# Second parts of weights by a ScalarE negation and an accumulating DMA in place of a subtraction, between the two layers of a decoder trunk

## The chip, the core and the metric

The program runs on one core of a Trainium2 chip. The metric is the device time of one execution in microseconds (us), lower is better. The engines are TensorE (PE in the rows, PEld for its weight loads), VectorE (DVE), ScalarE (ACT), GpSimd (POOL) and SyncE (SP, which only issues DMAs here). Each engine takes its instructions in the order in which they stand in its queue and waits at each for the semaphores that the instruction needs.

## What is computed

A trunk of two layers over 1024 tokens of 1024 channels, float32. Each layer is a token mixer and a squared-ReLU MLP with a hidden width of 4096, both behind an RMSNorm whose scale, shift and gate come from a conditioning vector. Layer 0 mixes with a recurrent block, layer 1 with a causal pooling mixer.

```
for i in (0, 1):
    h = rms_norm(x, g_mix[i]) * (1 + scale_m) + shift_m
    y = recurrent_mixer(h) if i == 0 else pool_mixer(h)
    x = x + gate_m * y
    h = rms_norm(x, g_ffn[i]) * (1 + scale_f) + shift_f
    u = relu(h @ w1[i])
    x = x + gate_f * ((u * u) @ w2[i])
return rms_norm(x, g_final)

# pool_mixer: four groups of 256 channels, windows of 2, 4, 8, 16 tokens
pooled = trailing_mean(h, window) - h
mixed = pooled @ w_pool[group]            # 256 x 256 each, times pool_scale
```

## The kernel before

The tokens are cut into two halves of 512 and the channels into blocks of 128, so that every tile is 128 partitions by 512 tokens. All weights and activations that TensorE takes are in two float32r parts that add up to the float32 value: a high part (the value cast to float32r) and a low part (the value less its high part). A product of one weight block with one activation block is three matmuls, all in `mm3`: high by high (L178), high by low (L179), low by high (L180).

A weight tile `w_...` of the pool `wpool` (eight buffers) holds both parts of 128x512 weights. A unit of 128x1024 weights is loaded by one DMA of SP into a `raw_...` tile (`load`, L99, three buffers) and made into two such tiles by `split_part`: ScalarE casts (L170), and GpSimd or VectorE, by the argument `eng`, subtracts (L171). A cast can run as soon as the last matmul that reads the buffer's former weights is through.

```
def split_part(raw, name, eng=None):
    w, n = split_tile(name), raw.shape[-1]
    S.copy(w[:, 0, 0:n], raw)                                                   # L170
    (eng or V).tensor_sub(w[:, 1, 0:n], raw, w[:, 0, 0:n].bitcast(F32))         # L171
    return w
```

Between the layers the halves of the tokens are run one behind the other, so that TensorE has the MLP of one half to do during the norm and the windows of the other. The order in which the program is written there is: `f2_fast(0, 6)` in two parts (`f2_weights_one`, then `f2_weights_two`), `f1` and `f2` of chunk 7 for the first half, `pool_windows(0)` spread as side work over the next products, `f1(0, 7, (1,))`, `pool_mix(0)`, `f2(0, 7, (1,))` with `ffn_norm(1, 0)` as side work, `pool_windows(1)` over `f1(1, 0, (0,))` and `f2(1, 0, (0,))`, `pool_mix(1)`, `f1(1, 1, (0,))` with `ffn_norm(1, 1)`, `f1(1, 0, (1,))`, `f2(1, 0, (1,))`. `f1` and `f2` are the first and second product of the MLP, with `f1_block` making the two parts of the squared hidden channels (`relu` L620, `usq` L625, `u` L609 and L610).

From that the framework's scheduler makes one fixed order for each engine and sets the semaphores; the order within a queue is not changed while the program runs. It puts casts far ahead of their use, as far as the eight buffers allow.

Names that the prediction uses: `pool_windows` makes the trailing sums `pw` (L900; windows of 16 on GpSimd, the others on VectorE), `pooled` (L907, L909, L910, L939), and the parts `ph` (ScalarE, L914) and `pl` (VectorE, L915). `SumSq.add` squares a block on ScalarE (L252) and adds it to a running sum on VectorE (L253: `ssqf1a`, `ssqn0b`, `ssqf1b`), which TensorE adds up over the partitions (L262). `norm_split` makes `hh` and `hl` (L284 to L291, three of eight `hl` on GpSimd at L288). `add_scaled` of `f2_fast` adds on GpSimd (L779).

Of the kernel before, what the change touches and what calls it, by code (L numbers as in the profile page):

```python
# [10 lines left out]
F32 = mybir.dt.float32  # L11
F32R = mybir.dt.float32r
AF = mybir.ActivationFunctionType
ALU = mybir.AluOpType
# [14 lines left out]
# Columns of the packed per-channel vectors, eight columns (one per block of channels) each.  # L29
# [13 lines left out]
def trunk_kernel(ctx, tc, xT, vecs, wmod, w_k, w_in, w_y, w_g, w_out, w_p, w1, w2, outT):  # L43
# [16 lines left out]
    class Blocks:  # L60
        """Eight blocks of channels of one half of the tokens, in two slots"""
# [41 lines left out]
    # The weights of the first products, in the order in which they are used: two blocks of rows  # L103
    # of six blocks of the input projection, and the conditioning's blocks of columns.
    mod_raw, k_raw = {}, []

    def piece(r, q, part):
        """Columns of a part of r, which is halved for the first two blocks of rows."""
        n = r.shape[-1] // (2 if q == 0 else 1)
        return part * n, part * n + n  # L110
# [29 lines left out]
    # silu(c) as a row on every partition  # L140
    cs = const.tile([P, NB], F32, name="cs")
    with tc.issue_after(S.activation(cs, vcol("c"), AF.Sigmoid).ins):
        # has the table of the first norm's square root loaded ahead of it
        S.activation(const.tile([P, 1], F32, name="early"), eps, AF.Sqrt)
# [3 lines left out]
    for n in range(2):  # L148
        ps = small_ps()
        # the columns of cs on diagonals, whose sums over the partitions are on every partition  # L150
        dg = tmp("dg").rearrange("p (q i) -> p q i", i=P)
        V.tensor_mul(dg, ident[:, None, :].to_broadcast([P, 4, P]),
                     cs[:, 4 * n:4 * n + 4, None].to_broadcast([P, 4, P]))
        PE.matmul(out=ps, lhsT=ones, rhs=dg, start=True, stop=True)
        cond_copy.append(S.copy(cond[:, n * H:(n + 1) * H], ps))
# [4 lines left out]
    def split_unit(src, name, eng=None, drips=None):  # L160
        raw = load(src, name)
        drip(rate[0] if drips is None else drips)
        return [split_part(raw[:, c:c + H], f"{name}_{c}", eng) for c in (0, H)]
# [10 lines left out]
    def mm3(ps, unit, col, rh, rl, first, last):  # L174
        """ps += unit[:, col:col+128].T @ (rh + rl)"""
        w, c = unit[col // H], col % H
        wh = w[:, 0, c:c + P]
        PE.matmul(out=ps, lhsT=wh, rhs=rh, start=first, stop=False)  # L178
        PE.matmul(out=ps, lhsT=wh, rhs=rl, start=False, stop=False)  # L179
        PE.matmul(out=ps, lhsT=w[:, 1, c:c + P], rhs=rh, start=False, stop=last)  # L180

    def proj(unit, hh, hl):
        """One 128-row block of W.T @ h for one token half, K = 1024."""
        ps = acc_mm()
        for k in range(NB):
            mm3(ps, unit, k * P, hh[:, k, :], hl[:, k, :], k == 0, k == NB - 1)
        return ps

# [6 lines left out]
    def mod_column(m, e, raw):  # L195
        """m[:, e] = raw @ cond"""
        V.scalar_tensor_tensor(raw, raw, 1.0, cond, op0=ALU.mult, op1=ALU.mult, accum_out=m[:, e:e + 1])  # L197
# [8 lines left out]
    def mod_steps():  # L206
        """The rest of the conditioning in small steps, taken between those of the other work."""
# [19 lines left out]
    def norm_scale(g, m, name):  # L227
        """g * (1 + scale)"""
# [5 lines left out]
    class SumSq:  # L234
        """Sums of squares of n tokens: up to three partial sums, added up by the tensor engine."""
# [19 lines left out]
    def rstd_bcast(ss, trace=None):  # L255
        """PSUM tile [P, n] with 1/sqrt(mean + eps) of every token on every partition."""
# [10 lines left out]
        # in two float32r parts on diagonals, whose sums over the partitions are on every partition  # L267
# [38 lines left out]
    # Six blocks of the input projection take the channels of the first half of the tokens  # L306
    # as the conditioning of each 128 of them is ready.
# [8 lines left out]
    def after(f, *args, **kw):  # L316
        """Issues behind what the last call on the same engine issued."""
# [7 lines left out]
    def column(dst, j, k, scale, first):  # L325
        """dst[:, k] = first + scale * (conditioning of channel block k)"""
# [16 lines left out]
    def prepare(q, part=0):  # L343
        """The float32r parts of the weights of two blocks of rows, or of one if q is 0"""
# [126 lines left out]
    # coefficient of the gate in log a: 8 * log_sigmoid(lambda)  # L471
# [17 lines left out]
    # log1p(z) = 2 s (1 + po)  # L489
# [11 lines left out]
    def gates(hd, unit, h):  # L501
        """RG-LRU of one head; its states take the place of its input."""
# [16 lines left out]
        for mi in range(2):  # L519
            b = 2 * hd + mi  # L520
            # a = exp(log a);  1 - a^2 = (1 + a^2) * tanh(-log a)
# [77 lines left out]
    # U[c]: the hidden channels of chunk c, in slots of two blocks each: (first or last two blocks,  # L599
    # half of the tokens), and the sums of them that the second product of the MLP takes  # L600
# [3 lines left out]
    def f1_block(unit, j, h, u, fast):  # L604
# [7 lines left out]
        def minus(a, n):  # L612
            """a less a block that is there in its two parts"""
# [15 lines left out]
        # for f2_fast the halves of the tokens change places  # L629
# [33 lines left out]
    class Ahead:  # L663
        """Units of weights, which are prepared one ahead of those in use"""
# [11 lines left out]
    # pieces of the conditioning by unit of a chunk of the MLP  # L676
# [8 lines left out]
    def f1(i, c, halves, by_half=False, eng=None, side=iter(()), fast=False, ahead=None):  # L685
        """`side` is other work, a step of which is traced after each unit.

        `fast` is set where f2_fast takes the result: "in turn" if one half of the tokens is done before the other.
        """
# [22 lines left out]
    def f2_weights(i, c, r, eng=None):  # L712
        """The parts of blocks of rows r and r + 4 of W2.T for f2_fast, by the product that takes them"""
# [18 lines left out]
    def f2_weights_one(i, c, r, eng):  # L732
        """Those of f2_weights for the products that the first half of the tokens takes"""
# [12 lines left out]
    def f2_weights_two(i, c, r, eng):  # L746
        """The others"""
        raw = rawp.tile([P, D + 256], F32, tag="raw", name=f"raw_w2_{i}_{c}_{r}")[:, 0:H]
        nc.sync.dma_start(raw, w2[i, c, r, :, 256:768])
        w = split_part(raw, "a12_a22", eng)  # L750
        return {2: (w, 0, (1, 0)), 4: (w, 256, "t4")}

    def f2_fast(i, c, ahead, products=(1, 5, 6, 3, 7, 2, 4), side=iter(())):
        """The second product of the MLP by Winograd's form of Strassen's seven products.

        W2.T is cut into two blocks of rows r, r + 4 by the first and last two hidden blocks, and the
        hidden channels into the latter by the halves of the tokens.
        """
# [52 lines left out]
        for r in range(4):  # L811
            # the last block of hidden channels is of use to the last two only
# [4 lines left out]
    # blocks of columns of a unit of w2, by block of rows of the product  # L817
# [22 lines left out]
    def once(fn):  # L840
        """Work of a single step"""
        fn()
        yield
# [3 lines left out]
    def jobs(i, first, last):  # L847
        """The units of chunks that run one after the other"""
# [14 lines left out]
    # 1 / min(t + 1, window) for the first 16 tokens  # L863
# [9 lines left out]
    def pool_windows(h, ss):  # L873
# [3 lines left out]
        def normed(k, hx, scale=1.0):  # L877
            """scale * (normalized and modulated x), after the last 15 tokens of the half before"""
# [46 lines left out]
        def ahead(k):  # L925
            if k < 6:
                hxs[k] = tmp("hx", W)
                # windows of two need only half the difference of neighbours, none for the first token
# [22 lines left out]
    def pool_mix(h, parts, out_ss):  # L951
        ph, pl = parts
        up = [split_unit(w_p[q], f"p{q}", G) for q in range(2)]
# [11 lines left out]
    # The first half of the tokens runs ahead of the second through the pooling mixer,  # L965
    # so that the tensor engine has one half's MLP to do during the other's norms and windows.
# [10 lines left out]
    f1(0, 7, (0,))  # L977
    f2(0, 7, (0,), sa)
    side = pool_windows(0, sa)
    f2_fast(0, 6, Ahead([partial(f2_weights_two, 0, 6, r, G) for r in range(4)]), (2, 4), side)  # L980
    f1(0, 7, (1,), eng=G, side=side)
# [3 lines left out]
    f2(0, 7, (1,), sb, eng=G, side=once(lambda: ffn_norm(1, 0, qa)))  # L985
    side = pool_windows(1, sb)
    f1(1, 0, (0,), eng=G, side=side)
    f2(1, 0, (0,), eng=G, side=side)
# [3 lines left out]
    f1(1, 1, (0,), eng=G, side=once(lambda: ffn_norm(1, 1, qb)), fast="in turn")  # L992
    f1(1, 0, (1,), eng=G)
    f2(1, 0, (1,))
# [28 lines left out]
    def mid_norm():  # L1023
        """The middle piece's final norm on GpSimd, which leaves VectorE to the last piece."""
# [19 lines left out]
def _layout(inputs):  # L1044
    """The arrays of the launch: the inputs, cut into the tiles that the kernel loads."""
# [28 lines left out]
    # two blocks of rows each: of the first 512 columns, then of the next 256  # L1074
# [3 lines left out]
    # two blocks of rows of the product each, r and r + 4  # L1078
# [34 lines left out]
```

## Time and profile before

| what | value |
|---|---|
| median of 3 runs | 1798.73 us (1798.16 to 1800.46) |
| span of the profiled execution | 1797.3 us |
| TensorE busy | 1718.5 us, 96% |
| VectorE busy | 1419.8 us, 79% |
| ScalarE busy | 913.7 us, 51% |
| GpSimd busy | 585.9 us, 33% |
| bytes moved by DMA | 158.76 MB, 88 GB/s over the span |

The profiled execution has no time beside its span; the median of the runs is 1.4 us longer than that span. Shares over the whole span say little here: between 360 and 990 us and from 1170 us on TensorE is nearly never idle, and what other engines save there is worth nothing. What counts is the stage between the layers, from about 990 to 1170 us, which is read by windows, waits and single instructions. A window's row gives its length, then for TensorE, its weight loads, VectorE, ScalarE and GpSimd the busy time and, in brackets, how many instructions ran; then the granted TensorE clock as a share of its upper level (1.00 is 2.4 GHz, 0.50 is 1.2 GHz), the busy share of the 16 DMA engines and GB/s.

### The profile page before, as it was taken

The page shows a single profiled execution, that of the slowest core. Times are in us where ns is not written, and L with a number is a line of the kernel's source. Part 1 is how long each engine was busy: PE and PEld are TensorE (multiplying, and loading weights), DVE is VectorE, ACT ScalarE, POOL GpSimd, SP SyncE. Part 2 cuts the span into 40 slices and gives each one's busy share as a digit, 9 for nine tenths or more (in the row PEclk, how much of TensorE's full clock was granted, in tenths as well). Part 3 has the DMA queues.
Part 4 walks back from the last instruction along what each step waited for, and adds up shares of the span by engine and source line. Part 5 has one row for each costly group of instructions (what it writes and reads, how often), then busy time and mean ns, then how long its engine had stood idle before and what let it go on. Part 6 is the DMA issues. An engine that isn't in the chain of part 4 may idle for free.

```text
span 1797.3 us, 20872 instructions
## 1 busy us (share of the span) xinstructions
PE 1718.5 (96%) x7510; PEld 1405.2 (78%) x7510; DVE 1419.8 (79%) x2124; ACT 913.7 (51%) x1558; POOL 585.9 (33%) x434
## 2 busy tenths in 40 slices
PE   6899989989999999999999988999999999999997
PEld 4687768778788888888888766788887787878787
DVE  8997866678888889898876897958787878686836
ACT  4588884255454444545454464445444444545422
POOL 5323341242322414151324655511322324041403
PEclk8999989989999999999999988999999999999999
DMA  9223314521424233242213221231202111121202
GB/s 363 73 84 109 136 47 142 162 83 59 136 70 134 73 115 106 94 126 73 83 58 106 81 72 59 83 105 51 70 33 71 36 59 52 42 61 46 71 13 94
DMA packets 47479, 158.76 MB, mean 88 GB/s; under 512 B 5008, under 2 KB 7440, under 8 KB 47376
## 3 DMA queue, kind: packets, MB, share of 16 engines
q1 hardware_dynamic: 47376, 157.43, 26.9%
q8 instruction: 59, 0.97, 0.2%
q14 instruction: 44, 0.36, 0.1%
HBM read 153.21 MB, written 4.19 MB: 88 GB/s over the span
## 4 chain that ended last, share of the span: by engine, by line
PE 62%; DVE 22%; ACT 5%; issue 5%; DMA 4%; POOL 2%; DVEq 0%; SPq 0%; ACTq 0%; POOLq 0%
PE mm L178 20%; PE mm L179 20%; PE mm L180 20%; DMA mb<-in_wmod 3%; DVE mb L197 2%; DVE xa L770 1%; DVE mw L323 1%; POOL xa L779 1%; DVE pw L900 1%; DVE xb L770 1%; DVE xca L439 1%; PE sm L262 1%; DVE hl L291 1%; DVE w_a_s L171 1%; DVE xcb L439 1%
## 5 line engine op out<-in xcount | busy, mean ns | idle before, releaser
L178 PE MATMUL mm<-hh,w_w 128*128 128x512 f32 x1024 | 401.4, 392 | 0.9 <-DVE xa L770 0.9
L180 PE MATMUL mm<-hh,w_w 128*128 128x512 f32 x1024 | 400.9, 392 | 0.0
L179 PE MATMUL mm<-hl,w_w 128*128 128x512 f32 x1024 | 400.6, 391 | 0.0
L779 POOL TENSOR_TENSOR xb<-xb,c 128x512 f32<-128x512 f32 x104 | 150.4, 1446 | 632.1 <-ACT c L774 564.4
L178 PEld LDWEIGHTS mm<-hh,w_w 128*128 128x128 f32 x1024 | 193.5, 189 | 42.8 <-DVE xa L770 2.7
L180 PEld LDWEIGHTS mm<-hh,w_w 128*128 128x128 f32 x1024 | 193.6, 189 | 40.3
L179 PEld LDWEIGHTS mm<-hl,w_w 128*128 128x128 f32 x1024 | 193.5, 189 | 40.0
L779 POOL TENSOR_TENSOR xa<-xa,c 128x512 f32<-128x512 f32 x104 | 160.3, 1542 | 145.1 <-ACT c L774 145.1
L774 ACT ACTIVATE c<-c,mod 128x512 f32<-128x512 f32 x104 | 75.3, 724 | 209.7 <-DVE c L800 119.8
L197 DVE SCALAR_TENSOR_TENSOR mb<-mb,cond 128x1024 f32<-128x1024 f32 x80 | 113.8, 1423 | 55.2 <-DMA mb<-in_wmod 54.6
L620 ACT ACTIVATE relu<-mm 128x512 f32<-128x512 f32 x128 | 76.2, 595 | 152.4 <-PE mm L180 143.6
L170 ACT CAST w_w<-raw_w 128x512 fp32r<-128x512 f32 x192 | 113.5, 614 | 63.2 <-PE mm L180 50.6
L171 DVE TENSOR_TENSOR w_w<-raw_w,w_w 128x512 fp32r<-128x512 f32 x136 | 130.5, 967 | 16.8 <-ACT w_w L170 16.7
L770 DVE SCALAR_TENSOR_TENSOR xa<-mm,mod,xa 128x512 f32<-128x512 f32 x156 | 112.9, 741 | 16.6 <-POOL xa L779 16.6
L171 POOL TENSOR_TENSOR w_w<-raw_w,w_w 128x512 fp32r<-128x512 f32 x56 | 83.5, 1498 | 71.6 <-ACT w_w L170 62.6
L179 PE MATMUL mm<-u,w_w 128*128 128x512 f32 (+1 forms) x224 | 81.4, 363 | 1.7 <-DVE u L610 1.7
L178 PE MATMUL mm<-u,w_w 128*128 128x512 f32 (+1 forms) x224 | 80.8, 364 | 1.7 <-ACT u L609 1.7
L180 PE MATMUL mm<-u,w_w 128*128 128x512 f32 (+1 forms) x224 | 81.0, 362 | 0.0
L178 PE MATMUL mm<-u,w_a_a 128*128 128x512 f32 x200 | 79.1, 396 | 1.9 <-DVE xa L770 1.0
L610 DVE TENSOR_TENSOR u<-usq,u 128x512 fp32r<-128x512 f32 x102 | 72.9, 715 | 8.5 <-ACT u L609 7.5
L770 DVE SCALAR_TENSOR_TENSOR xb<-mm,mod,xb 128x512 f32<-128x512 f32 x104 | 77.0, 741 | 2.6 <-PE mm L180 2.2
L179 PE MATMUL mm<-u,w_a_a 128*128 128x512 f32 x200 | 78.0, 390 | 0.0
(332 smaller groups left out, 4078.3 us busy)
## 6 DMA issues: line engine op xcount, KB each, us to landing
raw_w<-in_w SPq DMA_DIRECT2D x148, 512.0 KB, 3.6
mb<-in_wmod SPq DMA_DIRECT2D x80, 512.0 KB, 3.6
mw<-in_wmod SPq DMA_DIRECT2D x16, 512.0 KB, 9.6
raw_in<-in_w_in SPq DMA_DIRECT2D x8, 512.0 KB, 3.7
raw_y<-in_w_y SPq DMA_DIRECT2D x8, 512.0 KB, 3.6
raw_o<-in_w_out SPq DMA_DIRECT2D x8, 512.0 KB, 3.7
outT<-o SPq DMA_DIRECT2D x12, 256.0 KB, 2.4
xa<-in_xT SPq DMA_DIRECT2D x4, 512.0 KB, 5.4
```

The lines of the kernel that those rows point to most:

```text
L170: S.copy(w[:, 0, 0:n], raw)
L171: (eng or V).tensor_sub(w[:, 1, 0:n], raw, w[:, 0, 0:n].bitcast(F32))
L178: PE.matmul(out=ps, lhsT=wh, rhs=rh, start=first, stop=False)
L179: PE.matmul(out=ps, lhsT=wh, rhs=rl, start=False, stop=False)
L180: PE.matmul(out=ps, lhsT=w[:, 1, c:c + P], rhs=rh, start=False, stop=last)
L197: V.scalar_tensor_tensor(raw, raw, 1.0, cond, op0=ALU.mult, op1=ALU.mult, accum_out=m[:, e:e + 1])
L439: V.scalar_tensor_tensor(o, xr[:, k:k + H], vcol(f"cw{k}", m), o, op0=ALU.mult, op1=ALU.add)
L610: eng.tensor_sub(u[n][:, 1, jj, :], src, u[n][:, 0, jj, :].bitcast(F32))
L620: S.activation(r, ps, AF.Relu)
L770: V.scalar_tensor_tensor(xb, ps, g[:, r + 4 * row:r + 4 * row + 1], xb, op0=ALU.mult, op1=ALU.add)
L774: S.activation(t, src, AF.Identity, scale=g[:, r + 4 * row:r + 4 * row + 1])
L779: G.tensor_add(xb, xb, t)
```

## The change

For 84 of the weight tiles the low part is no longer a subtraction. ScalarE writes the high part as before, then writes its negative into the low part's place, and a DMA issued from GpSimd's queue reads the same weights from HBM a second time and adds them there: low = -high + value. The DMA is 256 KB, 128 rows of 2 KB. It waits for the negation, and the matmuls at L180 wait for its landing. Sixty of the 84 tiles had their subtraction on GpSimd, and 24 (chunk 7's `f1` and `f2` for the first half of the tokens, and `f2(1, 0, (1,))`) on VectorE. Beyond these tiles nothing changes its arithmetic. Comments and docstrings are taken out as well, and lines from `neg_part` on stand ten further down in the changed kernel.

```diff
+    def neg_part(raw, src, name):
+        w, n = split_tile(name), raw.shape[-1]
+        S.copy(w[:, 0, 0:n], raw)
+        S.activation(w[:, 1, 0:n], w[:, 0, 0:n].bitcast(F32), AF.Identity, scale=-1.0)
+        nc.gpsimd.dma_start(w[:, 1, 0:n], src, accum_op=ALU.add)
+        return w
     def split_unit(src, name, eng=None, drips=None):
         raw = load(src, name)
         drip(rate[0] if drips is None else drips)
+        if eng == "dma":
+            return [neg_part(raw[:, c:c + H], src[:, c:c + H], f"{name}_{c}") for c in (0, H)]
         return [split_part(raw[:, c:c + H], f"{name}_{c}", eng) for c in (0, H)]
...
-    def f2_weights_two(i, c, r, eng):
+    def f2_weights_two(i, c, r):
...
-        w = split_part(raw, "a12_a22", eng)
+        w = neg_part(raw, w2[i, c, r, :, 256:768], "a12_a22")
...
-        up = [split_unit(w_p[q], f"p{q}", G) for q in range(2)]
+        up = [split_unit(w_p[q], f"p{q}", "dma") for q in range(2)]
...
-    f1(0, 7, (0,))
-    f2(0, 7, (0,), sa)
+    f1(0, 7, (0,), eng="dma")
+    f2(0, 7, (0,), sa, eng="dma")
     side = pool_windows(0, sa)
-    f2_fast(0, 6, Ahead([partial(f2_weights_two, 0, 6, r, G) for r in range(4)]), (2, 4), side)
-    f1(0, 7, (1,), eng=G, side=side)
+    f2_fast(0, 6, Ahead([partial(f2_weights_two, 0, 6, r) for r in range(4)]), (2, 4), side)
+    f1(0, 7, (1,), eng="dma", side=side)
...
-    f2(0, 7, (1,), sb, eng=G, side=once(lambda: ffn_norm(1, 0, qa)))
+    f2(0, 7, (1,), sb, eng="dma", side=once(lambda: ffn_norm(1, 0, qa)))
     side = pool_windows(1, sb)
-    f1(1, 0, (0,), eng=G, side=side)
-    f2(1, 0, (0,), eng=G, side=side)
+    f1(1, 0, (0,), eng="dma", side=side)
+    f2(1, 0, (0,), eng="dma", side=side)
...
-    f1(1, 1, (0,), eng=G, side=once(lambda: ffn_norm(1, 1, qb)), fast="in turn")
-    f1(1, 0, (1,), eng=G)
-    f2(1, 0, (1,))
+    f1(1, 1, (0,), eng="dma", side=once(lambda: ffn_norm(1, 1, qb)), fast="in turn")
+    f1(1, 0, (1,), eng="dma")
+    f2(1, 0, (1,), eng="dma")
```

GpSimd's queue in `pool_windows(0)`, around the sums of the second block with a window of 16 (`pwork`, `pw`); `w_w1_0_7_3` is a unit of `f1(0, 7, (1,))`, `w_p0` one of `pool_mix(0)`. Before:

```order
L171 TENSOR_TENSOR w_w1_0_7_3_0_8227<-raw_w1_0_7_3_8225,w_w1_0_7_3_0_8227 128x512
L900 TENSOR_TENSOR pwork_7966<-hx_7955 128x526
L900 TENSOR_TENSOR pwork_7966<-pwork_7966 128x524
L900 TENSOR_TENSOR pwork_7966<-pwork_7966 128x520
L900 TENSOR_TENSOR pw_7975<-pwork_7966 128x512
L171 TENSOR_TENSOR w_w1_0_7_3_512_8230<-raw_w1_0_7_3_8225,w_w1_0_7_3_512_8230 128x512
L171 TENSOR_TENSOR w_p0_0_8297<-raw_p0_8295,w_p0_0_8297 128x512
```

The same piece of the queue in the changed kernel:

```order
L165 DMA w_w1_0_7_3_0_8253<-in_w1 128x512
L910 TENSOR_TENSOR pwork_7984<-hx_7973 128x526
L910 TENSOR_TENSOR pwork_7984<-pwork_7984 128x524
L910 TENSOR_TENSOR pwork_7984<-pwork_7984 128x520
L910 TENSOR_TENSOR pw_7993<-pwork_7984 128x512
L165 DMA w_w1_0_7_3_512_8257<-in_w1 128x512
L165 DMA w_p0_0_8325<-in_w_p 128x512
```

Each subtraction's place in the queue is taken by the issue of a DMA, and the sums stand where they stood.

ScalarE's queue a little later, ahead of `f2(0, 7, (1,))`, whose first unit is `w_w2_0_7_0`; `relu`, `ph` and `u01` belong to `f1_block` and to `pool_windows(0)`. Before:

```order
L170 CAST w_p1_512_8308<-raw_p1_8303 128x512
L886 ACTIVATE hx_8085<-nt_8086,mod1_0_3550 128x512
L888 COPY tail_6996<-hx_8085 128x15
L170 CAST w_w2_0_7_0_0_8400<-raw_w2_0_7_0_8398 128x512
L620 ACTIVATE relu_8144<-mm_8119 128x512
L914 CAST ph0_0_7951<-pooled_8095 128x512
L609 CAST u01_8101<-usq_8146 128x512
L170 CAST w_w2_0_7_0_512_8403<-raw_w2_0_7_0_8398 128x512
```

The same piece in the changed kernel:

```order
L163 CAST w_p1_512_8339<-raw_p1_8333 128x512
L924 CAST ph0_0_7969<-pooled_8083 128x512
L896 ACTIVATE hx_8105<-nt_8106,mod1_0_3550 128x512
L164 ACTIVATE w_p1_512_8339<-w_p1_512_8339 128x512
L898 COPY tail_6996<-hx_8105 128x15
L163 CAST w_w2_0_7_0_0_8432<-raw_w2_0_7_0_8430 128x512
L164 ACTIVATE w_w2_0_7_0_0_8432<-w_w2_0_7_0_0_8432 128x512
L630 ACTIVATE relu_8168<-mm_8143 128x512
L924 CAST ph0_0_7969<-pooled_8115 128x512
L619 CAST u01_8121<-usq_8170 128x512
L163 CAST w_w2_0_7_0_512_8436<-raw_w2_0_7_0_8430 128x512
L164 ACTIVATE w_w2_0_7_0_512_8436<-w_w2_0_7_0_512_8436 128x512
```

A negation stands behind each cast, and the rest of the queue keeps its order but for a place or two. TensorE's queue is the same in both kernels except for some neighbouring products that change places, and SP's is the same.

## Rows read from the trace of the kernel before

**Rows 1.** The page: busy time of each engine, share of the span.

```profile
PE 1718.5 (96%) x7510; PEld 1405.2 (78%) x7510; DVE 1419.8 (79%) x2124; ACT 913.7 (51%) x1558; POOL 585.9 (33%) x434
```

**Rows 2.** Windows around and in the stage; columns as above.

```profile
945.00:990.00 45.00, 45.00 (x199) 36.85 (x198) 27.66 (x38) 21.82 (x37) 20.01 (x15) 1.00 0.35 107
1170.00:1215.00 45.00, 45.00 (x200) 36.97 (x199) 24.19 (x34) 19.37 (x34) 6.05 (x5) 1.00 0.29 94
...
1030.00:1050.00 20.00, 13.31 (x34) 8.88 (x34) 19.26 (x32) 9.73 (x18) 8.27 (x6) 0.66 0.25 79
1065.00:1080.00 15.00, 15.00 (x68) 12.42 (x67) 14.91 (x19) 11.29 (x20) 11.27 (x8) 1.00 0.24 76
1080.00:1095.00 15.00, 10.62 (x35) 8.50 (x34) 9.29 (x15) 5.05 (x12) 4.45 (x3) 0.66 0.18 65
1105.00:1120.00 15.00, 11.60 (x43) 8.80 (x42) 13.38 (x16) 7.05 (x14) 7.59 (x5) 0.89 0.21 70
1135.00:1150.00 15.00, 11.85 (x42) 8.47 (x41) 14.93 (x20) 6.60 (x12) 8.10 (x5) 0.89 0.22 72
```

**Rows 3.** TensorE's waits, 1000 to 1180 us: us in total, times, longest.

```profile
PE mm L178 <- DVE usq L625: 4.9, 1, 4.9
PE sm L262 <- DVE ssqn0bV L253: 4.4, 1, 4.4
PE mm L178 <- ACT ph L914: 1.9, 1, 1.9
PE mm L179 <- DVE u L610: 1.7, 1, 1.7
```

**Rows 4.** VectorE's timeline: start, us taken, instruction, count, idle time before it.

```profile
1014.20 1.69 DVE L900 TENSOR_TENSOR pw<-hx 128x526 f32<-128x526 f32 x1
...
1019.33 1.14 DVE L909 TENSOR_TENSOR pooled<-pw,icnt 128x16 f32<-128x16 f32 x1
1020.50 0.18 DVE L910 TENSOR_TENSOR pooled<-pooled,hx 128x16 f32<-128x16 f32 x1
...
1028.31 0.70 DVE L900 TENSOR_TENSOR pw<-hx 128x526 f32<-128x526 f32 x1
...
1029.53 3.47 DVE L900 TENSOR_TENSOR pw<-pw 128x524 f32<-128x524 f32 x2
...
1035.23 0.68 DVE L625 SCALAR_TENSOR_TENSOR usq<-mm,relu 128x512 f32<-128x512 f32 x1
...
1050.56 0.75 DVE L962 SCALAR_TENSOR_TENSOR xa<-mm,gp,xa 128x512 f32<-128x512 f32 x1 [1.24 <-PE mm L180]
```

**Rows 5.** GpSimd's timeline in the same stretch.

```profile
1013.57 1.75 POOL L171 TENSOR_TENSOR w_w<-raw_w,w_w 128x512 fp32r<-128x512 f32 x1
1015.28 5.16 POOL L171 TENSOR_TENSOR w_p<-raw_p,w_p 128x512 fp32r<-128x512 f32 x3
```

**Rows 6.** Groups of instructions, 890 to 1220 us: busy us, mean ns, idle before.

```profile
L171 POOL TENSOR_TENSOR w_w<-raw_w,w_w 128x512 fp32r<-128x512 f32 x48 | 71.9, 1505 | 63.8 <-ACT w_w L170 54.8 <-issue 8.2 <-POOL hl L288 0.4
...
L253 DVE TENSOR_TENSOR ssqn0bV<-ssqn0bV,sq 128x512 f32<-128x512 f32 x7 | 8.9, 1270 | 0.2
L900 DVE TENSOR_TENSOR pw<-pw 128x524 f32<-128x524 f32 x8 | 10.0, 1249 | 0.3
```

**Rows 7.** DMA issues, 900 to 1220 us: count, KB, median us to landing.

```profile
raw_w<-in_w SPq DMA_DIRECT2D x42, 512.0 KB, 3.5
...
raw_w<-in_w SPq DMA_DIRECT2D x4, 256.0 KB, 2.8
```

**Rows 8.** ScalarE's and TensorE's timeline: first cast and first use of chunk 7's weights.

```profile
935.64 1.12 ACT L170 CAST w_w<-raw_w 128x512 fp32r<-128x512 f32 x2
...
948.12 0.39 PE L178 MATMUL mm<-hh,w_w 128*128 128x512 f32 x1
```

**Rows 9.** ScalarE's waits, 1000 to 1180 us: us in total, times, longest.

```profile
ACT w_w L170 <- PE mm L180: 20.7, 14, 3.9
ACT ph L914 <- DVE pooled L907: 12.4, 4, 5.0
```

## The prediction

> **What bounds the kernel now.** The page's busy times come first [rows 1]: TensorE works 1718.5 of 1797.3 us, so at most some 79 us can be had anywhere, and what counts is where TensorE stands still. The windows show where [rows 2]. Before and behind the stage between the layers (945 to 990, 1170 to 1215 us) TensorE is busy in all of its 45 us at a granted clock of 1.00, its upper level (2.4 GHz): time saved there on another engine is worth nothing. The window 1065 to 1080 gives the full rate, 68 matmuls in 15 us or 4.53 per us. Four windows fall short of it: 34 matmuls in 20 us (1030 to 1050) are 12.5 us too few, 35 in 15 us are 7.3, 43 are 5.5 and 42 are 5.7. Together 31.0 us are lost there, stalls and the lower clock behind them in one: the clock is 0.66 to 0.89 in these windows, a mean of both levels.
>
> TensorE's own waits name whom it waits for [rows 3]: `usq` of VectorE 4.9 us, `ssqn0bV` of VectorE 4.4, `ph` 1.9, `u` 1.7. So VectorE is late; it is busy 19.26 of 20 us and 14.93 of 15 us in two of the short windows, GpSimd and ScalarE about half of theirs [rows 2]. The last question is why VectorE is late. Its timeline beside GpSimd's tells [rows 4, 5]: the same instruction, L900 on 128x526, takes 1.69 us at 1014.20, while GpSimd subtracts (1013.57 to 1020.4), and 0.70 us at 1028.31, when GpSimd is idle; from 1029.53 two take 3.47 us, beside two more subtractions. A 128x16 operation of L909 takes 1.14 us, and L910 of that size right behind it 0.18. Instructions of VectorE that read two SBUF operands are held for as long as a subtraction of GpSimd runs. The subtractions are on no queue that TensorE waits for; they act through VectorE.
>
> **What the change takes away.** In the stretch 890 to 1220 GpSimd makes 48 subtractions of 1505 ns, 71.9 us [rows 6], the p units aside. With them goes what they hold. Window by window:
>
> 1030 to 1050, 12.5 us lost. TensorE stands from about 1031.0 until `usq` ends at 1035.9 (4.9 us, rows 3; start 1035.23 plus 0.68, rows 4), then runs at the lower clock. Between 1014.20 and 1031.4 eight of VectorE's instructions are stretched, seven of them to about 1.68 us (first and last in rows 4) in place of 0.70, one to 1.14 in place of 0.18: 6.9 + 1.0 = 7.9 us. `usq` then starts up to 7.9 us earlier, about 1027.4, ahead of the 1031.0 at which TensorE wants it. That wait goes, and with it the fall of the clock. Next late is VectorE again, which in before has no idle time until 1050.56 [rows 4]; I keep 3 us for it. Saved: 9.5.
>
> 1080 to 1095, 7.3 us lost, 4.4 of them the wait on `ssqn0bV` [rows 3]. Seven of these sums take 1270 ns [rows 6]; at 0.70 they are 4.0 us shorter, about the wait. Saved with the clock: 5, and 2.3 kept for the sum itself, which TensorE needs whole.
>
> 1105 to 1120, 5.5 us lost over `u`, `ph` and others. `u` depends on ScalarE's `relu` and on PSUM as well. Saved: 2.5, about half.
>
> 1135 to 1150, 5.7 us lost, VectorE at 14.93 of 15. Eight of L900 at 1249 ns [rows 6] are 4.4 us too long. Saved: 4.5.
>
> Sum 21.5 us. The bounds are 0 (no relief) and all 31.0.
>
> The 24 subtractions that VectorE loses stand where TensorE is at its full rate (chunk 7 for the first half, before 990; `f2(1, 0, (1,))`, behind 1170 [rows 2]): worth nothing, and so is the lighter GpSimd in itself.
>
> **What the change adds.** First, 84 negations of 128x512 on ScalarE. No such row stands in before; the nearest is the cast of the same tile, two in 1.12 us [rows 8], so some 0.52 us each where they follow one another. 29 of the 84 stand in the four short windows or just ahead of them: 29 x 0.52 = 15 us if all were on the path, nothing if all fall into gaps. ScalarE has gaps: it works 9.73 of 20 us and at most 11.29 of 15 [rows 2], and waits itself, 20.7 us for TensorE to free weight buffers and 12.4 for `pooled` [rows 9]. A negation stands right behind its cast, and a cast's wait is the usual one, so it mostly fills a gap. But `relu` and `ph` stand behind negations and VectorE and TensorE wait for these. I take 2 us, near the lower end, by the busy share.
>
> Second, a DMA from GpSimd's queue, issued in the place of each subtraction. The trace shows none. Bounds for GpSimd's own time from the row it replaces: 0 to 1.5 us. The queue's order is unchanged, so its sums (L910 in the changed kernel) and `hl` can come no later than now by this, unless a DMA's wait holds them; each waits for the negation, some 0.5 us behind the cast for which the subtraction waited. I cost it at nothing, covered by GpSimd's idle half.
>
> Third, the landing. The matmul L180 now waits for cast, negation, issue and transfer in place of cast and subtraction. A plain 256 KB takes 2.8 us to landing and 512 KB 3.5 [rows 7], so 0.7 us per 256 KB and 2.1 fixed. With 0.5 for the negation and 1 to 1.5 for the issue the low part comes 5 to 8 us behind its cast, if the addition costs a second pass or two. The first weights of chunk 7 are cast at 935.64 and used at 948.12 [rows 8], 11.4 us from the cast's end, the shortest such distance that I found among these tiles; most are 18 to 27. So it is covered, by 3 us at the tightest place; without that cover each late tile would cost its lateness.
>
> Whether the issue itself holds VectorE as the subtraction did, no row tells: bounds are full relief and none. I take full relief, since the instructions that are held read two operands, which points at reading, and an issue does not read the 128x512 operands as the subtraction did.
>
> The Trainium skill, page "SBUF — State Buffer", section "Who interferes with whom", has the same split: a VectorE instruction with two SBUF inputs contends with a GpSimd instruction that reads SBUF, not with one that only writes it. The trace agrees with the first half (1.69 against 0.70 us [rows 4]); the second half no row here shows.
>
> **Sum.** 21.5 - 2 = 19.5 us; 1797.3 - 19.5 = 1777.8 us of span; the median of the runs lies 1.4 us above the span: 1779.2 us.
>
> **The rivals.**
>
> *The issue holds VectorE as the subtraction did.* Slower than before. No relief, and the negations add 0 to 15 us: 1799 to 1814, about 1806. For it: GpSimd's time per issue could be as long as the subtraction. Against it: the held instructions are those that read two operands, which speaks of reading. It decides if the issue's hold on VectorE is over about 90% of the subtraction's.
>
> *Descriptors in VectorE's gaps.* VectorE has hardly a gap between 1028.31 and 1050.56 [rows 4]. If GpSimd can issue only while VectorE is idle, weights due in that stretch come up to 23 us late, and less the cover of 11.4 a wait of some 12 us takes the place of the one removed, there and once more in 1135 to 1150, against some 12.5 us saved: about 1809. Nothing in the trace speaks for it, since GpSimd's subtractions do start while VectorE works.
>
> The Trainium skill tells of such a case, page "SBUF — State Buffer", section "SBUF: two separate sides", in its box on VectorE blocking a DMA: GpSimd cannot write descriptors while VectorE runs an instruction in a mode that takes both ports; no run here shows it yet.
>
> *The accumulating DMA is too slow as a stream.* A tile has 12 matmuls, 12 / 4.53 = 2.65 us of TensorE. By 0.7 us per 256 KB a plain transfer is far from that; at three times, 2.1, it still fits; at 4 us per tile it does not: 60 or so tiles in a row lose 1.4 us each, 84 us, about 1880. If the DMAs went one after the other at three times their latency, 8.4 us, it would be 84 x (8.4 - 2.65), some 480 us and about 2280. The price per tile at which it decides is about 3. Against it: the DMA engines are busy at most 0.35 of the windows [rows 2].
>
> *Less comes back.* VectorE is shorter but ScalarE's `relu` and `ph`, now behind negations, are late next: 5 to 12 us saved, 1787 to 1794; or nothing net, 1797 to 1801.
>
> **How the numbers follow.** The forecast, 1770 to 1788, has 0.60; less comes back, 0.10; nothing net, 0.08; the issue holds VectorE, 0.13; descriptors in gaps, 0.03; the stream too slow, 0.06. A measurement of this kernel can tell about 0.2%, 3.6 us. Faster by more than that: 0.70, within it 0.08, slower 0.22. The range begins at all 31 us recovered, 1798.7 - 31 = 1767, and ends at 1814, where no relief meets all negations on the path; the slow stream lies outside.
>
> **What would show it.** Right: in the changed kernel TensorE's waits on `usq` and `ssqn0bV` are gone or under 1 us, its clock is 1.00 in 1030 to 1050, `ssqn0bV` and L910's `pw` on VectorE are back to about 0.7 us, no wait of TensorE names the DMA of L165, ScalarE is busy about 45 us more, GpSimd's subtractions are gone, and the 256 KB additions land within 3 to 5 us. Wrong: long two-operand instructions on VectorE beside an issue; `relu` or `ph` late behind negations; matmuls L180 that wait for L165; DMA engines full, or issues that wait for a gap of VectorE.

## The result and the profile after

| | before | after |
|---|---|---|
| median of the runs, 4 each | 1798.45 us (1797.14 to 1800.46) | 1768.76 us (1767.0 to 1770.3) |
| span of the profiled execution | 1797.3 us | 1766.5 us |
| TensorE busy | 1718.5 us | 1704.8 us |

The ratio is 0.9833 (95% interval 0.982 to 0.9847): 29.7 us faster, where 19.5 were forecast. The time lies inside the forecast's outer range (1767 to 1814 us), near its low end, and 1.2 us below the 1770 to 1788 us that had a chance of 0.60. The spans differ by 30.8 us, and the forecast's own count of what the four windows lose was 31.0.

The windows of the changed kernel show all of it back. The columns are those of [rows 2]; the pieces of the stage lie earlier, since time was won on the way.

```profile
945.00:990.00 45.00, 45.00 (x199) 36.91 (x198) 16.18 (x25) 30.91 (x54) 27.94 (x28) 1.00 0.98 217
...
1020.00:1040.00 20.00, 19.49 (x86) 15.53 (x85) 19.37 (x40) 15.88 (x29) 6.29 (x8) 1.00 0.97 219
1085.00:1100.00 15.00, 14.02 (x62) 11.16 (x61) 13.81 (x20) 10.11 (x22) 6.67 (x7) 1.00 0.68 140
1100.00:1120.00 20.00, 20.00 (x90) 16.54 (x89) 19.81 (x32) 15.45 (x29) 7.65 (x9) 1.00 0.97 226
```

In 20 us of the stage's first stall before had 34 matmuls at a mean granted clock of 0.66 [rows 2]; now there are 86 at 1.00 (1020 to 1040; 1030 to 1050 is at 1.00 too), with VectorE as busy as before (19.37 of 20 us): it does more in the same time. What is left of TensorE's waits, 980 to 1160 us, is the whole list (us in total, times, longest):

```profile
PE mm L188 <- ACT u L619: 1.0, 1, 1.0
PE sm L272 <- DVE ssqn0bV L263: 0.8, 1, 0.8
PE mm L188 <- DVE xa L972: 0.4, 1, 0.4
```

2.2 us in place of 19.0 us over all rows of the same view of before, of which [rows 3] shows the longest. That is 16.8 of the 30.8 us. The other 14 go with the clock, 0.66 to 0.89 in the four windows of before and 1.00 in all of after's: TensorE's busy time falls by 13.7 us (table above), for the same 7510 instructions. No row names L165, the DMA.

Why VectorE is in time shows in its timeline (start, us, instruction), the same pieces as in [rows 4]:

```profile
1014.90 0.69 DVE L910 TENSOR_TENSOR pw<-hx 128x526 f32<-128x526 f32 x1
...
1024.41 1.43 DVE L910 TENSOR_TENSOR pw<-pw 128x524 f32<-128x524 f32 x2
...
1028.11 0.69 DVE L635 SCALAR_TENSOR_TENSOR usq<-mm,relu 128x512 f32<-128x512 f32 x1
```

L910 takes 0.69 us where L900 took 1.69, two of them 1.43 where they took 3.47, and `usq` starts at 1028.11 in place of 1035.23, 7.1 us earlier. Beside the two that took 3.47 us (from 1029.53), GpSimd was subtracting in before:

```profile
1029.05 3.39 POOL L171 TENSOR_TENSOR w_w<-raw_w,w_w 128x512 fp32r<-128x512 f32 x2 [4.11 <-ACT w_w L170]
```

GpSimd's timeline after has issues right beside the first of these sums, and they don't stretch it:

```profile
1014.36 0.89 POOL L165 DMA_DIRECT2D w_w<-in_w  x1
1014.94 2.10 POOL L165 DMA_DIRECT2D w_p<-in_w_p  x2
```

The groups of 870 to 1200 us (count | busy us, mean ns | idle) say the same for the stage:

```profile
L165 POOL DMA_DIRECT2D w_w<-in_w x72 | 63.9, 923 | 85.2 <-ACT w_w L164 48.2 <-PE mm L190 20.3 <-issue 6.2
...
L263 DVE TENSOR_TENSOR ssqn0bV<-ssqn0bV,sq 128x512 f32<-128x512 f32 x7 | 4.8, 686 | 0.7 <-ACT sq L262 0.4
...
L620 DVE TENSOR_TENSOR u<-usq,u 128x512 fp32r<-128x512 f32 x25 | 17.3, 691 | 13.3 <-ACT u L619 13.3
```

`ssqn0bV` fell from 1270 ns [rows 6] to 686. The price of the change stands in the page and in its DMA part: ScalarE 958.9 us busy in place of 913.7, and a DMA queue that was not there, with landings of 6.0 us. The rows are queue, kind, packets, MB, share of 16 engines, then issue, count, KB, median us to landing, 880 to 1190 us:

```profile
q0 software_dynamic: 12096, 22.03, 42.9%
q1 hardware_dynamic: 7632, 26.74, 26.9%
...
w_w<-in_w POOLq DMA_DIRECT2D x72, 256.0 KB, 6.0
```

42.9% of 310 us for 84 tiles is 1.58 us of all 16 engines per addition; plain loads take 0.82 per 256 KB (26.9% of 310 us for 26.74 MB).

### The profile page after: what moved, and what is told of

Read it like the earlier page. It is cut to its first block, busy times and chain, and to the rows that moved or that the text cites. A ratio compares the mean times of both kernels' runs of the same rounds, so it can differ in the third digit from the quotient of the medians.

```text
span 1766.5 us, 20986 instructions
## 1 busy us (share of the span) xinstructions
PE 1704.8 (97%) x7510; PEld 1397.5 (79%) x7510; DVE 1370.7 (78%) x2100; ACT 958.9 (54%) x1642; POOL 566.6 (32%) x458
## 4 chain that ended last, share of the span: by engine, by line
PE 66%; DVE 19%; ACT 5%; issue 4%; DMA 4%; POOL 2%; SPq 0%; DVEq 0%; ACTq 0%; POOLq 0%
PE mm L188 22%; PE mm L189 22%; PE mm L190 21%; DMA mb<-in_wmod 3%; DVE mb L207 2%; DVE mw L333 1%; DVE xa L780 1%; DVE xb L780 1%; DVE xca L449 1%; DVE nt L294 1%; POOL xa L789 1%; DVE hl L301 1%; PE sm L272 1%; DVE xcb L449 1%; DVE w_s L181 1%
## 5 line engine op out<-in xcount | busy, mean ns | idle before, releaser
L181 DVE TENSOR_TENSOR w_w<-raw_w,w_w 128x512 fp32r<-128x512 f32 x112 | 109.1, 982 | 11.5 <-ACT w_w L180 11.5
L165 POOL DMA_DIRECT2D w_w<-in_w x72 | 63.9, 923 | 85.2 <-ACT w_w L164 48.2
L180 ACT CAST w_w<-raw_w 128x512 fp32r<-128x512 f32 x120 | 69.7, 612 | 29.1 <-PE mm L190 21.4
L620 DVE TENSOR_TENSOR u<-usq,u 128x512 fp32r<-128x512 f32 x102 | 70.4, 690 | 17.2 <-ACT u L619 16.8
```

The source lines that it names most:

```text
L165: nc.gpsimd.dma_start(w[:, 1, 0:n], src, accum_op=ALU.add)
L620: eng.tensor_sub(u[n][:, 1, jj, :], src, u[n][:, 0, jj, :].bitcast(F32))
```

## The experiments

The theory: the gain is VectorE, which is no longer held while GpSimd reads two operands for a subtraction; ScalarE's and the DMAs' work is covered. The rivals: that VectorE's own queue is 24 instructions shorter; that the weights come in another way; that any work of GpSimd holds VectorE; and, as to what is still to be had, that the DMA engines are nearly full. All ratios are to the kernel before, with 95% intervals.

**Each half of the change alone.** The first keeps the 24 subtractions of VectorE, the second the 60 of GpSimd.

```diff
-    f1(0, 7, (0,), eng="dma")
-    f2(0, 7, (0,), sa, eng="dma")
+    f1(0, 7, (0,))
+    f2(0, 7, (0,), sa)
...
-    f2(1, 0, (1,), eng="dma")
+    f2(1, 0, (1,))
```

> Only the 60 tiles that GpSimd subtracted are made by negation and accumulating DMA; the 24 that VectorE subtracted stay VectorE subtractions as before. Theory (the gain is VectorE released from GpSimd's two-operand reads): the whole gain stays, 1766 to 1772 us, and TensorE keeps a granted clock of 1.00 through the stage between the layers. Rival (the gain comes from VectorE's own queue being 24 instructions shorter): a good part of the 30 us is lost, 1780 to 1798.

Measured: 1769.9 us, 0.9843 (0.9824 to 0.9862): the whole gain, as far as the intervals tell.

```diff
-    f1(0, 7, (1,), eng="dma", side=side)
+    f1(0, 7, (1,), eng=G, side=side)
...
(and so for the other units and the four tiles of `f2_weights_two` that GpSimd subtracted before)
```

> The other half of the change alone: only the 24 tiles of VectorE by negation and DMA, the 60 of GpSimd subtracted on GpSimd as before. Theory: nothing, 1796 to 1801 us, the four short windows as before with VectorE's L253 and L910 sums still at about 1.25 us. Rival (VectorE's shorter queue): 1770 to 1790.

Measured: 1798.54 us, 1.0000 (0.9991 to 1.0009): nothing. TensorE's two longest waits are those of before, to the digit; `ssqn0bV` takes 1270 ns, as before, and the sums `pw` on VectorE take 1.14 to 1.38 us:

```profile
PE mm L188 <- DVE usq L635: 4.9, 1, 4.9
PE sm L272 <- DVE ssqn0bV L263: 4.4, 1, 4.4
```

So the gain is with the 60 tiles of GpSimd alone, and VectorE's shorter queue is worth nothing there, as forecast.

**Is it the reading?** Three kernels give GpSimd work back, behind each of the 60 issues, that nothing waits for: the old subtraction into a scratch tile; zeros written to it; and two subtractions of a constant tile, which keep no raw tile and no weight buffer.

```diff
+    scratch = const.tile([P, 256], F32, name="scratch")
...
         nc.gpsimd.dma_start(w[:, 1, 0:n], src, accum_op=ALU.add)
+        for c in (0, 256) if hold else ():
+            G.tensor_sub(scratch, raw[:, c:c + 256], w[:, 0, c:c + 256].bitcast(F32))
```

> The changed kernel, and behind each of the 60 DMA issues GpSimd makes the old subtraction once more, in two halves of 128x256, into a scratch tile that nobody reads: no weight depends on it. Theory (what counts is that GpSimd reads while VectorE reads two operands): VectorE's sums are stretched again to 1.1 us or more in the mean and most of the gain is lost, 1788 to 1802 us. Rival (the gain comes from the weights' way, from GpSimd's or VectorE's place in the chain of the weights): the gain stays, 1766 to 1773.

Measured: 1811.82 us, 1.0076 (1.0057 to 1.0095). All of the gain is lost and 13 us beyond it, 10 us above the theory's range. VectorE's sums are stretched again, as the theory had it (`ssqn0bV` 1160 ns).

```diff
+        with tc.issue_after(issue.ins):
+            for _ in range(4 if hold else 0):
+                G.memset(scratch, 0.0)
```

> The changed kernel, and behind each of the 60 DMA issues GpSimd fills the scratch tile with zeros, four times 128x256: it is busy in these places but reads nothing. Theory (reading is what holds VectorE): no change against the changed kernel, 1765 to 1773 us, VectorE's L910 and ssqn0bV sums stay near 0.70 us. Rival (any GpSimd work beside VectorE holds it): stretched sums, 1780 to 1802.

Measured: 1776.29 us, 0.9879 (0.9863 to 0.9896). Between the two: 7.5 us slower than the changed kernel, 3 us above the theory's range, with VectorE's sums not stretched at all (groups, 890 to 1220 us):

```profile
L170 POOL MEMSET scratch<- 128x256 f32 x240 | 97.4, 406 | 9.5
...
L915 DVE TENSOR_TENSOR pw<-pw 128x524 f32<-128x524 f32 (+1 forms) x12 | 8.4, 699 | 0.3
...
L268 DVE TENSOR_TENSOR ssqn0bV<-ssqn0bV,sq 128x512 f32<-128x512 f32 x7 | 4.8, 686 | 0.7 <-ACT sq L267 0.4
```

97.4 us of writing hold none of them. What it costs is mostly GpSimd's own work coming later (`ssqn0aG` is GpSimd's running sum): the last of these sums starts at 995.48 us, behind fills, where the changed kernel has it at 992.32. By the starts of the same product in both TensorE timelines, TensorE falls 5.0 us behind the changed kernel there, the wait and the lower clock (0.83, where it was 1.00) in one, and another 1.8 us near 1040, where it waits for `xa`. TensorE's waits, 980 to 1180 us, and the window:

```profile
PE mm L193 <- DVE xa L977: 2.0, 3, 0.8
PE sm L277 <- POOL ssqn0aG L268: 1.6, 1, 1.6
...
PE mm L195 <- DMA w_w<-in_w: 0.6, 1, 0.6
...
990.00:1010.00 20.00, 18.40 (x75) 15.14 (x74) 10.84 (x18) 9.04 (x17) 14.25 (x30) 0.83 0.64 140
```

```diff
+        with tc.issue_after(issue.ins):
+            for _ in range(2 if hold else 0):
+                G.tensor_sub(scratch, cond[:, 0:256], cond[:, 256:512])
```

> As the last two (work for GpSimd behind each of the 60 DMA issues, nothing depends on it), but now two subtractions of 128x256 of a constant tile: GpSimd reads two operands, and neither a raw tile nor a weight buffer is kept by it. Theory (GpSimd's reads hold VectorE): GpSimd's instructions and VectorE's two-operand sums stretch each other again, L910 and ssqn0bV on VectorE over 1.0 us in the mean, and the time comes to 1788 to 1806 us, well above the 1776.3 of the same places filled with zeros. Rival (what the copy of the subtraction cost came from the raw tiles that it held): 1774 to 1780, as with zeros.

Measured: 1813.63 us, 1.0088 (1.007 to 1.0107), as with the copy of the subtraction, and 8 us above the theory's range. The raw tiles were not the cause. In its groups (880 to 1220 us) reader and reader stretch each other, and TensorE's longest wait is that of before, longer:

```profile
L170 POOL TENSOR_TENSOR scratch<-cond 128x256 f32<-128x256 f32 x120 | 121.8, 1015 | 4.4
...
L915 DVE TENSOR_TENSOR pw<-pw 128x524 f32<-128x524 f32 (+1 forms) x12 | 12.5, 1042 | 0.3
...
L268 DVE TENSOR_TENSOR ssqn0bV<-ssqn0bV,sq 128x512 f32<-128x512 f32 x7 | 7.9, 1135 | 0.3
```

```profile
PE mm L193 <- DVE usq L640: 8.8, 2, 7.2
...
PE sm L277 <- POOL ssqn0aG L268: 0.7, 1, 0.7
```

Reading against writing, in the same places and with a quarter more time of GpSimd (121.8 against 97.4 us): 37 us. GpSimd's own lateness isn't what makes them, since TensorE waits less for `ssqn0aG` here than with the zeros (0.7 against 1.6 us), and VectorE less for GpSimd (7.4 against 12.7 us, 900 to 1220); an instruction of GpSimd that reads only one operand was not tried. Why both reading kernels come out slower than before, by 13 and 15 us, is not shown. A likely reason is GpSimd's time: 121.8 us, where the subtractions before took 90.4 (71.9 [rows 6], 13.3 for the p units and 5.2 for the `a12_a22` tiles), together with the 0.92 us of each issue ahead of them. A few instructions also stand elsewhere in these two kernels (by the traces 27 of ScalarE's 1642 and 2 of TensorE's 7510, against the changed kernel).

**ScalarE's part alone.** The negation stays, the subtraction comes back behind it, there is no DMA.

```diff
-        nc.gpsimd.dma_start(w[:, 1, 0:n], src, accum_op=ALU.add)
+        eng.tensor_sub(w[:, 1, 0:n], raw, w[:, 0, 0:n].bitcast(F32))
```

> The negation of all 84 tiles stays on ScalarE, but the low part is then written by the old subtraction on its old engine (GpSimd 60, VectorE 24) and there is no DMA: the kernel before with ScalarE's part of the change alone added. Theory: the negations fall into ScalarE's gaps, 0 to 4 us over before, 1798 to 1803. Rival (ScalarE's relu and ph come late behind them): over 1805. If it is faster than before, the negation's delay of the subtractions matters, which neither theory has.

Measured: 1800.02 us, 1.0009 (0.9999 to 1.0019): 84 negations of 628 ns cost 1.5 us beside the old subtractions, which the interval (up to 3.4) doesn't tell from nothing. The forecast took 2.

**What the DMA costs.** First plain DMAs in place of the accumulating ones.

```diff
-        nc.gpsimd.dma_start(w[:, 1, 0:n], src, accum_op=ALU.add)
+        nc.gpsimd.dma_start(w[:, 1, 0:n], src)
```

> The changed kernel with plain DMAs in place of the accumulating ones, in the same places and of the same bytes (the low part is then the whole weight, so the result isn't the reference's). Theory (the DMA is covered): the same time as the changed kernel, 1766 to 1771 us; the time of GpSimd's DMA queue falls from 1.58 us of all 16 engines per tile (42.9% of 310 us for 84) to about 0.8, and their landing from 6.0 to about 4 us. Rival (the addition's price is on the path): faster than the changed kernel by over 3 us.

Measured: 1767.1 us, 0.9829 (0.9813 to 0.9844), no difference that can be told from the changed kernel's 0.9833. The addition's price in the engines is there, but on no path: 25.9% of 310 us for 84 tiles is 0.96 us where the additions took 1.58, and an issue occupies GpSimd for 541 ns where it took 923. The landing falls from 6.0 to 3.6 us.

```profile
q0 software_dynamic: 12096, 22.03, 25.9%
...
L165 POOL DMA_DIRECT2D w_w<-in_w x72 | 38.9, 541 | 113.0 <-ACT w_w L164 91.7 <-PE mm L190 17.8 <-PE mm L188 2.6
...
w_w<-in_w POOLq DMA_DIRECT2D x72, 256.0 KB, 3.6
```

Then every addition twice, to find the limit.

```diff
         nc.gpsimd.dma_start(w[:, 1, 0:n], src, accum_op=ALU.add)
+        nc.gpsimd.dma_start(w[:, 1, 0:n], src, accum_op=ALU.add)
```

> The changed kernel with every accumulating DMA issued twice, one behind the other (the weight is then added twice, so the result isn't the reference's). The stream then needs 2 x 1.58 + 0.82 (the load) = 4.0 us of the DMA engines per tile, against 2.65 us of TensorE. Theory (the DMA engines are close to being the bound in the changed kernel, at a share of 0.98 in 945 to 990 us): TensorE waits for L165's landing, and the time rises by some 80 x 1.3 = 100 us less the cover, 1830 to 1890. Rival (the share of 0.98 is queueing and there is plenty of room): 1768 to 1785.

Measured: 1932.26 us, 1.0748 (1.0731 to 1.0765). Slower than either range. TensorE does wait for landings, though the share of the DMA engines (0.81 to 0.91 from 945 to 1340 us) lies below the changed kernel's 0.98. The second addition to the same tile waits until the first has landed, in GpSimd's queue, and everything behind it waits too. GpSimd's waits and TensorE's (900 to 1400 us):

```profile
POOL w_w L166 <- DMA w_w<-in_w: 124.2, 51, 6.3
```

```profile
PE mm L191 <- DMA w_w<-in_w: 60.8, 29, 4.7
PE sm L273 <- POOL ssqn0aG L264: 12.5, 1, 12.5
```

So this run prices a DMA's landing that is waited for in GpSimd's queue, and leaves the engines' limit open. For that the next two give the DMA engines more to move that nothing waits for.

```diff
+            with tc.issue_after(last_load[0].ins):
+                nc.sync.dma_start(junk[n_junk[0]], src)
```

> Doubling the additions also made each tile's two DMAs wait for one another and GpSimd's queue with them, so that run can't tell a full DMA stream from a long chain. Here the changed kernel stays as it is, and the DMA engines get more to do that nothing waits for: behind the load of each of the 40 units SyncE issues a copy of the same 512 KB from HBM to HBM. By the loads' price that is 0.8 us of all 16 engines more per tile, 1.58 + 0.82 + 0.8 = 3.2 us against 2.65 us of TensorE. Theory (the DMA engines are nearly full): TensorE waits for L165 and for raw tiles, 1785 to 1815 us. Rival (the share of 0.98 is packets that wait in line, and there is room): 1768 to 1775.

Measured: 2146.24 us, 1.1937 (1.1917 to 1.1957). It doesn't answer the question. Each copy came out as 16 packets of 32 KB, and the framework's scheduler planned another order: by the trace at least 224 of ScalarE's 1642 instructions stand elsewhere, and casts of weights stand behind instructions that wait (`relu` waits 171.9 us for TensorE). The DMA engines were at 0.26 to 0.57 in the stage, TensorE waited 177.1 us for additions that came late, and SyncE's loads waited 391 us for casts to free raw tiles:

```profile
SPq L101 <- ACT w_w L167: 391.0, 27, 25.4
```

The second form has rows that can't be merged; no other instruction of the changed kernel moves.

```diff
-    junk = nc.dram_tensor("junk", (44, P, D), F32, kind="Internal").ap()
+    junk = nc.dram_tensor("junk", (44, P, D + 64), F32, kind="Internal").ap()[:, :, 0:D]
```

> The extra copies of 512 KB behind each of the 40 units' loads once more, now to rows that don't lie end to end, with every other instruction of the five queues in the order of the changed kernel (in the first form of this run 419 of ScalarE's 1606 instructions stood elsewhere, so its time says nothing of the DMA engines). The stream then needs 1.58 + 0.82 + 0.8 = 3.2 us per tile against 2.65 us of TensorE. Theory (the DMA engines are nearly full in the changed kernel): TensorE waits for the landing of L165's additions and for raw tiles, some 84 x 0.55 = 46 us less a cover of 10 to 20: 1785 to 1815 us, DMA share near 1 throughout. Rival (the share counts packets that wait, there is room): 1767 to 1776.

Measured: 1772.2 us, 0.9851 (0.9835 to 0.9868): 3.4 us above the changed kernel, with intervals that overlap, and the theory that the DMA engines are nearly full falls. The landing of the additions went to 6.9 us, TensorE still waited for none of them, and 275 GB/s moved where it had been 217. A small price isn't excluded: in the profiled execution TensorE has one wait that it hasn't in the changed kernel, for `ssqn0aG`, whose last sum starts at 995.75 us in place of 992.32, behind an issue that waited 1.7 us for its negation. By the starts of the same product TensorE falls 4.9 us behind there. Windows, then the wait:

```profile
945.00:990.00 45.00, 45.00 (x199) 36.91 (x198) 15.68 (x25) 31.47 (x55) 25.99 (x27) 1.00 1.05 275
...
1100.00:1140.00 40.00, 40.00 (x181) 32.94 (x180) 34.46 (x56) 29.67 (x55) 13.06 (x15) 1.00 1.06 285
...
PE sm L279 <- POOL ssqn0aG L270: 1.3, 1, 1.3
```

**Other ways to the same end.** The 60 subtractions to VectorE, without negation or DMA:

```diff
-    f1(0, 7, (1,), eng=G, side=side)
+    f1(0, 7, (1,), side=side)
...
(and so for the other units of the 60)
```

> The simplest other way to take the subtractions off GpSimd: the 60 go to VectorE, no negation and no DMA. VectorE then has 60 x 0.69 = 41 us more of its own, some 34 of the 60 within 980 to 1180 us (23 us), and no hold by subtractions there (26 us by the difference of the sums' means). Theory (VectorE's time in the four windows is what counts, by whomever it is spent): about as before, 1785 to 1805 us. Rival (only the hold counts, extra instructions fall into gaps): 1768 to 1778.

Measured: 1792.47 us, 0.9962 (0.9948 to 0.9977): 7 us. The sums are at 696 and 680 ns here too, so the hold is gone as in the changed kernel, and most of what that gives is spent again on VectorE, where now a weight is late:

```profile
PE mm L180 <- DVE w_w L171: 9.8, 2, 8.4
PE mm L178 <- DVE xa L962: 4.7, 2, 2.8
```

And more of the same, for the first product of the other MLP chunks:

```diff
-            yield from f1_jobs(i, c, G if (i, c) == (0, 0) else None)
+            yield from f1_jobs(i, c, G if (i, c) == (0, 0) else "dma")
...
-        yield from f1_jobs(i, last)
+        yield from f1_jobs(i, last, "dma")
```

> The changed kernel, and the first product's weights of all other MLP chunks by negation and DMA too (104 more tiles, formerly VectorE's), to see whether more of the same gives more. There TensorE waits in all some 6 us on xa of VectorE (7 times, up to 1.0), which itself waits for GpSimd's additions. Theory (only where VectorE is late and held does the change pay): 1764 to 1772, no clear change, with GpSimd's queue fuller by 104 issues of 0.92 us. Rival (a lighter VectorE pays everywhere): 1755 to 1763; the DMA stream could also be too slow there: over 1775.

Measured: 1771.24 us, 0.9848 (0.9833 to 0.9863): no gain over the changed kernel, though VectorE is busy for 1290.4 us in place of 1370.7. The profiled execution has a new wait of 4.8 us for `xb` of VectorE near 465 us, whose cause wasn't followed; so the run shows that nothing is gained this way, not that a lighter VectorE is worth nothing there. No version here can be told to be faster than the changed kernel.

## Why the prediction was right, and where its sizes were off

*What bounds the kernel.* Right. The four windows and what follows right behind them held all that was to be had, VectorE was what TensorE waited for, and GpSimd's reads were why. The last is shown, not only argued: reads given back cost the gain (1813.63 us), writes in the same places don't stretch VectorE (699 ns).

*What the change takes away.* The mechanism was right and the size too small, 21.5 where about 31 came back. By the starts of the same product in both TensorE timelines, the four windows gave 11.6, 7.2, 4.3 and 5.9 us, where I forecast 9.5, 5, 2.5 and 4.5; the stretches right behind the first and the last gave 2.1 more. The term that was mis-sized is what I kept back in each window: 3 us in 1030 to 1050 for "VectorE again", 2.3 in 1080 to 1095, 3 of 5.5 in 1105 to 1120, 1.2 in 1135 to 1150, 9.5 in all. `usq` came 7.1 us earlier by the trace, or 7.8 with the 0.7 us by which the trace of after runs later up to there, against 7.9 by the sum, so that term was well sized. Behind it I took VectorE's unbroken run up to 1050.56 for work; it was work and holding (at 1037.72 us L910 on 128x16 took 1.29 us), and the same 19.4 us of VectorE now go with 86 matmuls. For 1105 to 1120 I credited half because `u` depends on ScalarE as well; but `u`'s own instruction on VectorE was stretched too (now 691 ns in the mean), and so was `pl` (839 ns in the mean, now 715):

```profile
1111.39 1.75 DVE L610 TENSOR_TENSOR u<-usq,u 128x512 fp32r<-128x512 f32 x1
```

And what I kept held a share of the loss by the lower clock: with 2.2 us of waits left the clock stays at 1.00, and none of that loss remains.

*The 24 subtractions of VectorE.* Right: worth nothing (1798.54 us alone).

*ScalarE.* Right: 45.2 us more busy, and about 1.5 us when alone, not to be told from nothing, against 2 forecast.

*The DMA.* Right in the sum, off in its parts. GpSimd's time per issue, bounded by 0 to 1.5 us, was 0.92. The landing, 6.0 us, was longer than the 3 to 5 I named as the sign of success, with the engines' share at 0.97 and 0.98; the cover held. A stream that should have been too slow from "about 3" us per tile was not: 3.2, counted with loads and copies, cost 3.4 us in all by the medians, where 84 tiles at 0.55 us would have been 46. That count took packet time for capacity.

*The rivals.* "The issue holds VectorE as the subtraction did" is out: 0.69 us beside issues. The Trainium skill's rule, page "SBUF — State Buffer", section "Who interferes with whom", that a VectorE instruction with two SBUF inputs does not contend with a GpSimd instruction that only writes SBUF, is now borne out in its second half by the zeros (686 and 699 ns). "Descriptors in VectorE's gaps" is out for this kernel: VectorE was busy 19.37 of 20 us and additions landed in 6.0 us; whether the mode of both ports that the prediction names would block the issues was not tried. "Less comes back" fell with the windows, "too slow as a stream" with the two loads.

## What to carry to other kernels

When the late engine shows one instruction at two durations, look at what runs beside the long ones: the cost of an engine with time to spare can lie on another engine's instructions, and its own waits and busy share don't show it. Ask of each piece of work not only which engine has room, but whose instructions it holds; here moving it to VectorE gave 7 us, and moving it off both gave 30. In this kernel the stalls and the lower clock behind them had one cause, and all that the windows lost came back: keep a share back only where a second late chain can be named with a row.

## What was not expected of the hardware

The busy share of the DMA engines is no measure of room: at 0.98 and 217 GB/s there was room for 275 GB/s, at a share of 1.05, for 3.4 us in all by the medians. An accumulating DMA keeps GpSimd for 923 ns at its issue, a plain one of the same 256 KB for 541, and takes 1.58 against 0.96 us of the engines. And an instruction that GpSimd makes for nobody is not free even if it holds nothing: 240 fills of 406 ns cost 7.5 us, most of it where a sum of GpSimd's own stands behind them.
